# One encoder step on one core: a planner in the kernel sets the order of issue on all five engines

## The chip, the cores and the metric

The kernel runs as one program on one core of a Trainium2 chip. The metric is device time in microseconds of one execution, lower is better. Engines: PE (matrix), DVE (vector), ACT (scalar, activation functions), POOL (general, element-wise here), SP (only issues DMAs). Each works through its own queue in the order in which it was filled; an instruction that waits holds up those behind it on that engine.

## The reference, cut to what matters

One layer of a streaming encoder over 2048 prompt and 32 sample tokens (2080 columns in the kernel), model width 1024, fp32:

```
h  = RMSNorm(x);  qa,ka,va, qb,kb,vb, g,r = split(h @ w_in)
oa = band_attention(qa, ka, va)         # 8 heads x 64, own 64-token chunk and 8 before it, learned bias
ob = GLA(qb, kb, vb, sigmoid(g @ w_alpha2)^(1/16))   # 4 heads, state 64 x 128, serial in time
x += RMSNorm(concat(oa, RMSNorm(ob) * silu(r)) @ w_o)
x += RMSNorm(cross_attention(RMSNorm(x), 256 memory tokens, 4 heads x 256))
x += RMSNorm((silu(h @ w_gate) * (h @ w_up)) @ w_down)     # hidden 2816
```

Outputs are x and the new caches (the last keys and values, the GLA state, memory keys and values).

## The kernel before

Activations are feature-major (features on partitions, tokens along the row). Each fp32 operand is split into a rounded part (ACT cast, `split`, L77) and a rest (subtract on DVE or POOL, L81); a product is then three matmuls (`mm3`, L136). The large products work on 2 x 2 blocks with seven products in place of eight: operands are combined first (`sub` and `add`, L180 and L183: `seven_mov` for activations, `seven_sta` for weights), and a *unit* accumulates the seven products in three PSUM banks X, Y and Z. X is read out after each of its products by an ACT copy or a DVE add (`out`, L222, which only raises the priority):

```
prod(X, w[0], m[0], True, True);  out(ACT.copy, cp[0], X)
prod(Y, w[1], m[1], True, True);  out(ACT.copy, cp[1], Y)
prod(X, w[2], m[2], False, True); out(ACT.copy, cp[2], X)
prod(Y, w[3], m[3], False, True); out(add, DVE, dst[0, 1], cp[2], Y)
```

Four phases follow one another, each with its own pools:

1. *Projection* (about 0 to 620 us of the profile): three token blocks, weights streamed (`wva`, `wvb`, `wqa`, `wka`, `wqb`, `wkb`, `wr`; `_r` is the loaded weight, `_s` its split), results stored to DRAM (`qd`, `kad`, `vad`, `vbd`, ...). Between them SP fills the unused rows of these with `ones` (L538) and `zero` (L545), and the bias table is made: `rb` is loaded (L549, L550), copied on DVE (L551) and expanded through DRAM (`biasd`, `fl`, `nbd`).
2. *Mixing* (620 to 1450): band attention in units (scores `s`, transposes `pt`, value products `po`), GLA in tiles of 128 tokens (`gla_tile`: `g_z` gate, `g_e` and `g_W` decay, `g_s` scores, `g_t`, `g_o` output, `g_st` state, `g_tt` transpose back, each step waiting for the one before), and the output projection of four blocks (`wops`, L991), which reads the attention result `om` back from DRAM (`od`). Memory keys and values and the first query product fill in.
3. *Cross attention* (1450 to 2030): five blocks of 416 tokens; `mqps` queries, `ms` scores (softmax on ACT and DVE, transposes `mpt`), `mpv` values, `mops` output projection, norm, then the feed-forward input `h2d` in DRAM.
4. *Feed-forward* (2030 to the end): three blocks of 2 x 348 or 346 tokens, in each 11 groups of a gate unit (`pg`), an up unit (`pu`) and the down product of the group before (`pdn`, L136, into the six PSUM banks that X, Y and Z use too), which DVE copies (first group, L222) or adds (L183) into `acc`. `acc` has two tiles for a block, and the pool has two buffers: a block's first copies need the buffers of the block before. When a block ends, `square` sums squares into `ssq` (ACT, DVE); `finish` of that block is run after the next block's first gate and up units: a matmul with ones (`n_ps`, L1540), Ln and Exp on ACT (`rstd_of`, L85 and L86, each with a table load), eight multiplies by gain and norm on DVE (L1547), eight adds of the residual on POOL, two stores of `y_t` (L1550). In the last group `ffn_ops` makes the next block's operands `mf`.

The program text says what runs; the order on each engine is set by the tile framework's scheduler (`schedule_with_timeline_sim=True`), which takes ready instructions by priority. The kernel shapes it with `tc.high_priority(offset=...)` around loads and splits (`PRI` = 4000), with `out` and with `weave`, which mixes lists of steps in the program.

## Time and profile before

| | us |
|---|---|
| runs (3), median | 3518.83 (3514.37 to 3520.55) |
| the profiled execution, its own time | 3519.91 |
| its span, first to last instruction | 3518.1 |
| PE busy / DVE / ACT / POOL | 3230.3 / 2258.6 / 1705.1 / 1541.9 |
| mean granted clock of PE | 0.956 |

In a line of the trace stand the start, the busy time of the group, engine, line, operation, output <- inputs, shapes and count, and in brackets how long the engine was idle before it and what released it. Names in the profile leave numbers out: `g_tt` is the g_tt of any tile, `n_ps` any block's. A window's clock is the mean granted clock of PE in it.

### The profile page before, as it was taken

The numbers are of one execution on the slowest core, as the hardware profiler recorded it, in microseconds if no ns is written. First come the engines' busy times: TensorE is split into PE (matmuls) and PEld (weight loads), VectorE is DVE, ScalarE is ACT, GpSimd is POOL, SyncE is SP. The second block draws the span as 40 slices with busy tenths as digits, with TensorE's granted clock in tenths as the row PEclk, the third lists the DMA queues.
The fourth block names the chain that finished last, engine by engine and source line by source line (L and its number), as shares of the span: only waits on it lengthen the run. The fifth ranks groups of instructions, "written<-read, shape, count | busy, mean of one in ns | idle before, by whom it ended". The sixth has DMA issues, their size and how long they took to land.

```text
span 3518.1 us, 58416 instructions
## 1 busy us (share of the span) xinstructions
PE 3230.3 (92%) x21387; PEld 3070.5 (87%) x21387; DVE 2258.6 (64%) x4089; ACT 1705.1 (48%) x3719; POOL 1541.9 (44%) x1331
## 2 busy tenths in 40 slices
PE   7788899899999799879999879999989999899998
PEld 6788899788887578869999769999989999899998
DVE  7774855576676567266566686555875556865555
ACT  4554645566665366345455443333543334543334
POOL 4543533353445445553434453333454334543332
PEclk8999999899999799989999989999999999999999
DMA  5448364877585566874655542222342222332222
GB/s 141 156 127 283 110 183 134 255 241 249 158 283 167 167 209 193 287 223 119 208 186 176 164 158 72 73 72 79 99 137 73 73 72 86 99 91 79 72 73 89
DMA packets 520112, 520.42 MB, mean 148 GB/s; under 512 B 81936, under 2 KB 450745, under 8 KB 519825
## 3 DMA queue, kind: packets, MB, share of 16 engines
q1 hardware_dynamic: 519825, 516.70, 47.5%
q8 instruction: 168, 2.75, 0.3%
q14 instruction: 119, 0.97, 0.1%
HBM read 386.82 MB, written 130.87 MB: 147 GB/s over the span
## 4 chain that ended last, share of the span: by engine, by line
PE 62%; DVE 11%; DMA 5%; ACT 3%; issue 3%; POOL 2%; SPq 1%; DVEq 0%; POOLq 0%; ACTq 0%
PE pdn L136 13%; PE pg_X L136 6%; PE pu_X L136 6%; PE mops L136 5%; PE wops L991 4%; PE pu_Y L136 3%; PE pg_Y L136 3%; PE po L715 2%; PE mqps L136 2%; PE pu_Z L136 2%; PE pg_Z L136 2%; PE s L710 1%; PE ms L136 1%; DVE y L1349 1%; PE mpv L136 1%
## 5 line engine op out<-in xcount | busy, mean ns | idle before, releaser
L136 PE MATMUL pdn<-u,wd 128*128 128x346 f32 (+1 forms) x3168 | 525.0, 323 | 12.6 <-DVE acc L183 9.6
L136 PEld LDWEIGHTS pdn<-u,wd 128*128 128x128 f32 x3168 | 509.0, 190 | 14.6 <-DVE acc L183 10.7
L77 ACT CAST wg_s<-wg_r 128x512 fp32r<-128x512 f32 x231 | 139.3, 620 | 341.2 <-PE pdn L136 194.9
L183 DVE TENSOR_TENSOR acc<-acc,pdn 128x346 f32<-128x346 f32 (+1 forms) x464 | 233.3, 512 | 97.4 <-PE pdn L136 97.2
L136 PE MATMUL pg_X<-mf,wg_s 128*128 128x346 f32 (+1 forms) x1584 | 280.0, 326 | 16.8 <-ACT wg_s L77 16.2
L136 PE MATMUL pu_X<-mf,wu_s 128*128 128x346 f32 (+1 forms) x1584 | 285.9, 324 | 10.1 <-DVE up L183 9.5
L136 PEld LDWEIGHTS pg_X<-mf,wg_s 128*128 128x128 f32 x1584 | 261.0, 192 | 18.9 <-ACT wg_s L77 17.0
L81 POOL TENSOR_TENSOR wu_s<-wu_r,wu_s 128x512 fp32r<-128x512 f32 x132 | 174.5, 1323 | 233.2 <-ACT wu_s L77 209.7
L136 PEld LDWEIGHTS pu_X<-mf,wu_s 128*128 128x128 f32 x1584 | 260.8, 191 | 11.8 <-DVE up L183 10.9
L81 POOL TENSOR_TENSOR u<-sg,u 128x346 fp32r<-128x346 f32 (+1 forms) x132 | 151.9, 1161 | 236.0 <-ACT u L77 236.0
L991 PE MATMUL wops<-om,wo_s 128*128 128x512 f32 (+1 forms) x960 | 216.5, 378 | 25.5 <-DMA om<-od 11.2
L81 POOL TENSOR_TENSOR wg_s<-wg_r,wg_s 128x512 fp32r<-128x512 f32 x99 | 136.1, 1376 | 233.4 <-ACT wg_s L77 233.3
L136 PE MATMUL mops<-mo,wmo_s 128*128 128x416 f32 x960 | 200.2, 360 | 15.0 <-ACT mo L1320 6.7
L991 PEld LDWEIGHTS wops<-om,wo_s 128*128 128x128 f32 x960 | 165.0, 204 | 54.6 <-DMA om<-od 11.9
L136 PEld LDWEIGHTS mops<-mo,wmo_s 128*128 128x128 f32 x960 | 180.1, 192 | 21.7 <-ACT mo L1320 7.7
L77 ACT CAST wu_s<-wu_r 128x512 fp32r<-128x512 f32 x231 | 136.4, 619 | 65.9 <-DVE wu_r L183 36.2
L136 PE MATMUL mqps<-m,wmq_s 128*128 128x416 f32 x768 | 161.5, 359 | 5.9 <-DVE wmq_s L81 5.9
L715 PE MATMUL po<-prt,v 128*128 128x128 f32 x1120 | 159.7, 286 | 6.6 <-ACT prt L744 4.3
L715 PEld LDWEIGHTS po<-prt,v 128*128 128x128 f32 x1120 | 147.5, 200 | 14.8 <-ACT prt L744 4.8
L81 DVE TENSOR_TENSOR wg_s<-wg_r,wg_s 128x512 fp32r<-128x512 f32 x132 | 102.3, 776 | 86.4 <-ACT wg_s L77 86.4
L136 PE MATMUL pu_Y<-mf,wu_s 128*128 128x346 f32 (+1 forms) x792 | 141.3, 327 | 14.3 <-ACT wu_s L77 14.3
L136 PEld LDWEIGHTS mqps<-m,wmq_s 128*128 128x128 f32 x768 | 143.3, 191 | 9.5 <-DVE wmq_s L81 6.9
(476 smaller groups left out, 7892.4 us busy)
## 6 DMA issues: line engine op xcount, KB each, us to landing
wg_r<-in_w_ffn_gate_dram SPq DMA_DIRECT2D x66, 512.0 KB, 4.4
wu_r<-in_w_ffn_up_dram SPq DMA_DIRECT2D x66, 512.0 KB, 3.8
wd_r<-in_w_ffn_down_dram SPq DMA_DIRECT2D x66, 512.0 KB, 3.5
wmq_r<-in_w_mq_dram SPq DMA_DIRECT2D x80, 256.0 KB, 2.9
wmo_r<-in_w_mo_dram SPq DMA_DIRECT2D x80, 256.0 KB, 3.2
q<-qd SPq DMA_DIRECT2D x32, 512.0 KB, 5.0
wo_r<-in_w_o_dram SPq DMA_DIRECT2D x64, 256.0 KB, 3.6
om<-od SPq DMA_DIRECT2D x24, 512.0 KB, 8.5
```

The costliest lines, as they stand in the source:

```text
L77: ACT.copy(hi, src)
L81: lo_eng.tensor_tensor(out=lo, in0=src, in1=hi.bitcast(F32), op=ALU.subtract)
L136: PE.matmul(ps, lhsT=a, rhs=b, start=first and i == 0, stop=last and i == len(seq) - 1, skip_group_check=skip)
L183: eng.tensor_tensor(out=out, in0=a, in1=b, op=ALU.add)
L710: PE.matmul(ps_out, lhsT=q[:, 2 * i + e, q0 : q0 + nq], rhs=ks[:, e, k0 : k0 + ncol], start=i == 0, stop=i == 1)
L715: PE.matmul(po[:, e * P : e * P + n], lhsT=v[:kk, j, e * 64 : e * 64 + P], rhs=prt[:kk, j, :n], start=j == 0, stop=j == len(rows) - 1)
L991: PE.matmul(ps, lhsT=a, rhs=b, start=i == 0, stop=i == len(seq) - 1)
L1349: DVE.scalar_tensor_tensor(out=y[k], in0=y[k], scalar=gains["g_post_mem"][:, k : k + 1], in1=r, op0=ALU.mult, op1=ALU.mult)
```

## The change

A class `Order` is added and called twice: it is made when the pools are opened, and `queue()` runs at the end of the program. It reads the traced instructions with their tiles, gives each a price by engine and size, and works out what each needs: earlier writers and readers of the same cells, a free buffer of its tag, the release of pools whose room is taken over. A pass then plays all five engines against each other: whenever an engine is free it takes the ready instruction of highest priority. The first pass uses the program's priorities; after each pass a backward pass works out how late each instruction could run, and this is the next priority; of four passes the one that ends first by its own clock is kept. Last, each engine's instructions (SP's DMAs too) are chained in the order of their planned starts by dependencies that need no semaphore, so the framework's scheduler has no choice left. The instructions themselves stay as they are. Table loads of ACT are in no price, DVE and POOL are priced alone, and PE always at one clock. All lines after the class move down by 327 (L1547 becomes L1874, L136 L463, L81 L408).

```diff
+class Order:
+    ENGINES = ("PE", "Activation", "DVE", "Pool", "SP")
+    GATE = 5
+    SLOW = 1.1
+    PASSES = 3
...
+    def _cost(self, ins, kind, eng, outs, inps):
+        n = self._free(outs[0])
+        slow = self.SLOW
+        if eng == "PE":
+            if any(a.tensor.name.startswith(("ident", "anti")) for a in inps):
+                return (max(30.0, n * 0.86) if n < 128 else 110.0), 250.0
+            if any(a.dtype == F32 for a in inps):
+                if n <= 64 and list(inps[0].ap)[0][1] <= 64:
+                    return 82.0, 300.0
+                return 2 * max(n * 0.84, 60.0 if n < 128 else 108.0), 300.0
+            t = n * 0.4385 + 6.5
+            return (max(t, 111.0 if n >= 128 else 60.0) if n < 256 else t), 250.0
+        if eng == "SP":
+            return 450.0, 2200.0
+        if kind == "InstMemset":
+            t = 60 + n * 0.5
+        elif eng == "Activation":
+            if kind == "InstActivation":
+                t = 170 + n * 0.9 + (195 if len(outs) > 1 else 0)
+            else:
+                t = 165 + n * (0.87 if outs[0].dtype == F32R else 0.82)
+        elif eng == "Pool":
+            t = 170 + n * 2.35
+        elif kind == "InstTensorCopy":
+            t = 150 + n * 1.05
+        elif kind == "InstTensorTensor":
+            t = 200 + n * 1.15
+        elif kind == "InstTensorReduce":
+            m = self._free(inps[0])
+            t = 60 + m * (1.95 if m > 2 * n else 1.0)
+        elif kind == "InstReciprocal":
+            t = 130 + n * 6.4
+        elif kind == "InstTensorScalarPtr":
+            t = 120 + n * 0.83 if len(inps) < 3 else (230 + n * 1.75 if n > 256 else 200 + n * 1.4)
+        else:
+            t = 245 + n * 1.05
+        return t * slow, 90.0
...
+    def _pass(self, prio, back=None):
...
+            again = True
+            while again:
+                again = False
+                for e, heap in enumerate(ready):
+                    while idle[e] and heap:
+                        _, i = heappop(heap)
+                        stop = None
+                        for k in self.uses[i]:
+                            g = self.tag[k]
+                            if not held[k] and (free[g] <= 0 or head[g] != place[k] or (back is None and self.first[k] != i)):
+                                stop = g
+                                break
...
+                        idle[e] = False
+                        start[i] = now
+                        fin = now + dur[i]
+                        heappush(events, (fin, 0, i))
+                        if back is None:
+                            seen = fin + lat[i]
+                            if e == 4:
+                                moved = max(moved, fin) + self.size[i] / 300.0
+                                seen = max(fin + 1900.0, moved + 1300.0)
+                            end[i] = seen
+                            heappush(events, (seen, 1, i))
+                        else:
+                            end[i] = fin
...
+    def queue(self):
+        self._read(self.block.bb.instructions)
+        n = len(self.ops)
+        best = None
+        prio = self.prio
+        for turn in range(self.PASSES + 1):
+            start, end = self._pass(prio)
+            if best is None or max(end) < best[0]:
+                best = (max(end), start)
+            if turn == self.PASSES:
+                break
+            back, fin = self._pass([-(s + d) for s, d in zip(start, self.dur)], back=end)
+            whole = max(fin)
+            prio = [whole - b for b in fin]
+        start = best[1]
+        tail = {}
+        for i in sorted(range(n), key=lambda i: (start[i], i)):
+            e = self.eng[i]
+            if e == self.GATE:
+                continue
+            if e in tail:
+                self.tc.add_manual_dep(self.ops[i], self.ops[tail[e]].name, self.edge, reason="order of issue")
+            tail[e] = i
...
     RW = dict(reuse_waits="tile")
 
+    issue_order = Order(tc)
     PRI = 4000
...
                 finish_rows(0, xts)
 
+    issue_order.queue()
```

Three places show what moves. First PE where GLA tile 11 ends and the output projection of token block 2 begins (names: g11_tt is the last transpose of tile 11; wops1_7 the last of eight column blocks of block 1; s, pt and po with numbers 10 to 13 are band attention). Before:

```order
L975 MATMUL g11_tt_13132<-ident_61,g11_ob_12971 128x128 x4
L895 MATMUL g12_e18_13165<-tall_6191,g12_laR_12851 128x128 x2
L1021 MATMUL sqa_1_ps0_13196<-acc1_1_11331,ones_63 128x512
L917 MATMUL g12_s0_13233<-g12_W0_12920 64x64
L922 MATMUL g12_s0_13233<-g12_W0_12920 64x64 x12
L922 MATMUL g12_s0_13233<-g12_kq_12643 64x64 x2
L917 MATMUL g12_s1_13234<-g12_W0_12920 64x64
L922 MATMUL g12_s1_13234<-g12_W0_12920 64x64 x12
L922 MATMUL g12_s1_13234<-g12_kq_12643 64x64 x2
L991 MATMUL wops2_0_0_13779<-om2_4_13668,wo2_0_4_s_13776 128x512 x3
```

In the new order the end of wops1_7, band attention and tile 12 stand around g11_tt:

```order
L1318 MATMUL wops1_7_0_12949<-om1_3_11325,wo1_7_0_s_12941 128x512
L1037 MATMUL s11_7_1_13114<-ks10_3_12758,q10_3_12756 128x320 x2
L1222 MATMUL g12_e10_13103<-tall_6191,g12_laR_12851 128x512 x2
L1222 MATMUL g12_e14_13107<-tall_6191,g12_laR_12851 128x512
L1037 MATMUL s12_0_0_13154<-ks12_0_13045,q12_0_13043 128x320 x2
L1222 MATMUL g12_e14_13107<-tall_6191,g12_laR_12851 128x512
L1042 MATMUL po10_3_13096<-prt10_6_13074,v10_3_12759 128x128
L1069 MATMUL pt10_7_0_13123<-ident_61,u10_7_sb_12989 128x128 x3
L1037 MATMUL s12_0_1_13157<-ks12_0_13045,q12_0_13043 128x320 x2
L1069 MATMUL pt10_7_3_13128<-ident_61,u10_7_sb_12989 128x128
L1302 MATMUL g11_tt_13132<-ident_61,g11_ob_12971 128x128 x4
L1069 MATMUL pt10_7_3_13128<-ident_61,u10_7_sb_12989 128x128
```

Before, tile 11 comes well after all of wops1, and with eight rows between them wops2 begins; now tile 11 ends right behind wops1_7, and the first wops2 stands 44 rows after g11_tt.

Second SP in the projection, from the second load of weight unit wka1_0 (the rb loads are the bias table). Before (the 8x384 load of rb stands further up):

```order
L336 DMA wka1_0_r1_2810<-in_w_fm_dram 128x1024
L457 DMA vad1_83<-wva1_st0_2091 128x2x64 x2
L538 DMA vad1_83<-ones_2422 512x1x64 x6
L538 DMA vad2_84<-ones_2422 512x1x64 x6
L538 DMA vad2_84<-ones_2422 128x1x64
L545 DMA qd0_67<-zero_2441 64x512
L478 DMA glow1_98<-wva1_low_2378 16x768
L545 DMA qd0_67<-zero_2441 64x512 x3
L336 DMA wka1_1_r0_2971<-in_w_fm_dram 128x1024
```

```order
L336 DMA wka1_1_r1_2973<-in_w_fm_dram 128x1024
L545 DMA qd1_68<-zero_2441 64x768 x7
L545 DMA qd2_69<-zero_2441 64x800 x7
L336 DMA wqb1_r0_3134<-in_w_fm_dram 128x1024
L545 DMA qd2_69<-zero_2441 64x800
L550 DMA rb_2467<-in_rel_rev_dram 8x1
```

Now (the second load of wka1_0 stands three rows, five stores of ones, further up):

```order
L865 DMA vad2_84<-ones_2422 512x1x64 x3
L865 DMA vad1_83<-ones_2422 512x1x64
L865 DMA vad2_84<-ones_2422 128x1x64
L872 DMA qd0_67<-zero_2441 64x512 x8
L872 DMA qd1_68<-zero_2441 64x768 x8
L872 DMA qd2_69<-zero_2441 64x800
L663 DMA wka1_1_r0_2971<-in_w_fm_dram 128x1024
L872 DMA qd2_69<-zero_2441 64x800 x2
L876 DMA rb_2467<-in_rel_rev_dram 8x384
L877 DMA rb_2467<-in_rel_rev_dram 8x1
L872 DMA qd2_69<-zero_2441 64x800 x5
L663 DMA wka1_1_r1_2973<-in_w_fm_dram 128x1024
```

The stores of ones and zeros go out in one stretch, the rb loads stand in it, and the two loads of wka1_1 behind most of it. On DVE the copy of rb now stands in the splits of wka1_0 (before, it stood in those of wka1_1):

```order
L507 TENSOR_TENSOR wka1_0_r0_2808<-wka1_0_r1_2810,wka1_0_r0_2808 128x4x128
L878 COPY rb_2467<-rb_2467 8x382
L815 SCALAR_TENSOR_TENSOR ql1_0_2602<-wqa1_0_st_2503,qh1_0_2601 128x768
L408 TENSOR_TENSOR wka1_0_s2_2821<-wka1_0_r0_2808,wka1_0_s2_2821 128x512
L507 TENSOR_TENSOR wka1_0_r0_2808<-wka1_0_r1_2810,wka1_0_r0_2808 128x4x128
```

So what DVE does for wka1_0 comes after rb has landed.

Third DVE at the change from feed-forward block 0 to block 1 (acc0_1 and acc0_0 are block 0's sums, n5_0_1_r its norm; pu1_0 and pu1_1 the first two up units of block 1, pdn1_0 its first down product). Before, all eight multiplies stand in one row in the first unit's reads:

```order
L81 TENSOR_TENSOR wg1_1_s0_27601<-wg1_1_r0_27597,wg1_1_s0_27601 128x512
L180 TENSOR_TENSOR wg1_1_r0_27597<-wg1_1_r0_27597 128x4x128
L183 TENSOR_TENSOR wg1_1_r0_27597<-wg1_1_r0_27597,wg1_1_r1_27599 128x4x128
L1547 SCALAR_TENSOR_TENSOR acc0_1_22591<-acc0_1_22591,g_post_ffn_849,n5_0_1_r_27563 128x348 x8
L180 TENSOR_TENSOR wg1_1_r0_27597<-wg1_1_r1_27599,wg1_1_r0_27597 128x4x128
L183 TENSOR_TENSOR up1_0_01_27290<-pu1_0_c2_27456,pu1_0_Y_27452 128x346
L1481 TENSOR_TENSOR sg1_0_01_27286<-sg1_0_01_27286,up1_0_01_27290 128x346
L81 TENSOR_TENSOR wg1_1_s2_27610<-wg1_1_r0_27597,wg1_1_s2_27610 128x512
```

Now they come one group later, right ahead of the first copies into block 1's sums:

```order
L1874 SCALAR_TENSOR_TENSOR acc0_1_22591<-acc0_1_22591,g_post_ffn_849,n5_0_1_r_27563 128x348
L510 TENSOR_TENSOR ssq0_0_27205<-ssq0_0_27205,sq0_0_5_27259 128x348
L1874 SCALAR_TENSOR_TENSOR acc0_1_22591<-acc0_1_22591,g_post_ffn_849,n5_0_1_r_27563 128x348 x2
L510 TENSOR_TENSOR ssq0_0_27205<-ssq0_0_27205,sq0_0_6_27270 128x348
L1874 SCALAR_TENSOR_TENSOR acc0_1_22591<-acc0_1_22591,g_post_ffn_849,n5_0_1_r_27563 128x348
L510 TENSOR_TENSOR ssq0_0_27205<-ssq0_0_27205,sq0_0_7_27281 128x348
L1874 SCALAR_TENSOR_TENSOR acc0_1_22591<-acc0_1_22591,g_post_ffn_849,n5_0_1_r_27563 128x348 x3
L507 TENSOR_TENSOR wg1_2_r0_28043<-wg1_2_r0_28043 128x4x128
L1808 TENSOR_TENSOR sg1_1_10_27593<-sg1_1_10_27593,pu1_1_X_27755 128x346
L1874 SCALAR_TENSOR_TENSOR acc0_0_22590<-acc0_0_22590,g_post_ffn_849,n5_0_0_r_27867 128x348 x5
L549 COPY acc1_1_27285<-pdn1_0_0_1_27908 128x346
```

The multiplies of acc0_1 are spread over the reads of pu1_1, and five of acc0_0 stand ahead of the first copy of pdn1_0.

213 lines of the change are left out of this document (added).

## Prediction

> **What bounds the kernel now.** I read the page's first part and the chain of waits, then busy time and granted clock by stretch, then the timeline of the places where PE stands still.
>
> ```profile
> PE 3230.3 (92%) x21387; PEld 3070.5 (87%) x21387; DVE 2258.6 (64%) x4089; ACT 1705.1 (48%) x3719; POOL 1541.9 (44%) x1331
> PE 62%; DVE 11%; DMA 5%; ACT 3%; issue 3%; POOL 2%; SPq 1%; DVEq 0%; POOLq 0%; ACTq 0%
> ```
>
> PE is busy for 3230.3 of 3518.1 us, and 62% of the chain that ended last lies on it. A different order can win only what PE does not use: 287.8 us without work, and time in which its clock is not granted in full. The stretches follow the program's phases (in a row: length, busy PE, PEld, DVE, ACT, POOL, clock, DMA share, GB/s).
>
> ```profile
> 0.00:310.00 310.00, 244.75 (x1596) 230.91 (x1597) 213.82 (x266) 149.88 (x287) 134.90 (x88) 0.90 0.56 163
> 310.00:620.00 310.00, 299.13 (x1874) 292.37 (x1873) 197.87 (x255) 166.28 (x308) 133.78 (x89) 0.98 0.52 162
> 620.00:1144.00 524.00, 483.37 (x4211) 425.32 (x4209) 346.50 (x990) 320.21 (x857) 237.07 (x319) 0.95 0.71 225
> 1144.00:1232.00 88.00, 63.53 (x454) 46.81 (x455) 51.67 (x116) 31.91 (x92) 40.15 (x55) 0.77 0.53 166
> 1232.00:1450.00 218.00, 196.27 (x1516) 170.31 (x1515) 133.02 (x345) 126.81 (x339) 115.49 (x125) 0.94 0.72 226
> 1450.00:2024.00 574.00, 519.99 (x2964) 493.15 (x2962) 346.73 (x574) 290.80 (x661) 249.43 (x180) 0.96 0.60 185
> 2024.00:2112.00 88.00, 66.83 (x354) 61.67 (x355) 72.26 (x86) 43.69 (x78) 46.59 (x32) 0.85 0.49 158
> 2464.00:2640.00 176.00, 158.31 (x947) 155.51 (x946) 141.71 (x186) 83.88 (x152) 92.57 (x65) 0.95 0.39 118
> 2904.00:3080.00 176.00, 158.43 (x948) 155.69 (x947) 138.57 (x186) 84.54 (x153) 90.97 (x64) 0.95 0.31 93
> 3432.00:3518.00 86.00, 71.73 (x454) 70.79 (x452) 46.38 (x78) 35.86 (x73) 22.66 (x19) 0.93 0.28 91
> ...
> sum 968.00, PE 968.00 PEld 968.00 DVE 570.08 ACT 371.28 POOL 378.31; mean PE 322.67 PEld 322.67 DVE 190.03 ACT 123.76 POOL 126.11
> ```
>
> Length minus busy PE is idle; busy times one minus the clock is about what the clock costs. Idle, then clock: 65.3 and 24 (0:310), 10.9 and 6, 40.6 and 24, 24.5 and 15 (1144:1232), 21.7 and 12, 54.0 and 21 (1450:2024), 21.2 and 10, 17.7 and 8 (2464:2640), 17.6 and 8 (2904:3080), 14.3 and 5. That is some 288 us idle and 133 us of clock. The last row sums the steady feed-forward groups (2112:2464, 2640:2904, 3080:3432): PE is busy for 968.00 of 968.00 us. Over a quarter of the span can give nothing, only lose.
>
> **The change part by part.** No work is added or removed; what moves is the place of each instruction in its queue, so every term is a wait that shrinks, stays or is new.
>
> *GLA beside w_o (1144:1232).* Rows: start, length, then what ended the wait.
>
> ```profile
> 1157.60 0.60 PE L975 MATMUL g_tt<-ident,g_ob 128*128 128x128 f32 x4
> 1183.49 0.60 PE L975 MATMUL g_tt<-ident,g_ob 128*128 128x128 f32 x4
> 1196.01 2.99 PE L991 MATMUL wops<-om,wo_s 128*128 128x512 f32 x6 [7.80 <-DMA om<-od]
> ```
>
> The last transposes of GLA tiles 10 and 11 (g_tt) are 1183.49 − 1157.60 = 25.9 us apart, and in that stretch PE has hardly anything but this serial chain: matmul, Exp, mask, matmul. After tile 11 the result goes through DRAM (od, then om), and the first w_o product of block 2 starts 1196.01 − 1183.49 = 12.5 us later; PE has 31 matmuls in between and then waits 7.80 us. In the new PE queue the z matmul of tile 10 stands in w_o's third column block of block 1 instead of at the end of its fifth, g11_z in the fourth instead of behind the seventh, and between g11_tt and wops2 stand 125 matmuls, most of them band attention. So tiles 10 and 11 run inside w_o and band work that before was spent earlier. Floor of the gain: 0, if dense work merely runs out later. Ceiling: the 39 us of idle and clock. I take 28: at the stretch's mean of 63.53/454 = 0.14 us the 125 matmuls are 17 us, but half of them are 64 wide and shorter, so I count 9 and leave 3 of the 12.5 us open; the other 8 are short waits inside the tiles.
>
> The same shift goes through 620:1144 and 1232:1450, where the tiles' waits are 1 to 5 us each. Bounds: 0 and 65, 0 and 34 us (a loss is the slower rival's). I take 12 and 8, a fifth to a quarter: the GLA chain stays serial, and the other waits there are for DMAs whose sources do not move.
>
> *Entry of cross attention.*
>
> ```profile
> 1573.36 0.61 PE L1308 MATMUL mpt<-ident,mpr 104*128 104x104 f32 x2 [7.08 <-ACT prT L1309]
> 1581.77 1.06 PE L136 MATMUL mops<-mo,wmo_s 128*128 128x416 f32 x2 [5.05 <-ACT mo L1320]
> ```
>
> Score matmuls (ms) of block 0 stand some 4 to 10 us of PE work further ahead of w_mo's first product than before. These two waits are 12.1 us; softmax in front of them stays. I take 10 here and 5 from the rest of 1450:2024, where the other blocks move less; bounds 0 and 30.
>
> *Projection, 0:310.* Here the new order also does harm.
>
> ```profile
> 247.35 0.46 SPq L336 DMA_DIRECT2D wka_r<-in_w_fm_dram  x1
> 248.91 11.13 SPq L538 DMA_DIRECT2D vad<-ones  x13
> 267.58 11.93 SPq L545 DMA_DIRECT2D qd<-zero  x14
> 281.00 0.49 SPq L550 DMA_DIRECT2D rb<-in_rel_rev_dram  x1
> 264.75 0.69 DVE L180 TENSOR_TENSOR wka_r<-wka_r,wka_r 128x512 f32<-128x512 f32 x1 [2.13 <-POOL wka_s L81]
> 285.00 0.35 DVE L551 COPY rb<-rb 8x382 f32<-8x382 f32 x1 [7.43 <-DMA rb<-in_rel_rev_dram]
> 291.44 4.21 PE L136 MATMUL wka_Z<-mi,wka_s 128*128 128x384 f32 x12 [10.72 <-DVE wqa_st L183]
> ```
>
> DVE's copy of rb waited 7.43 us for a load that SP issued behind ones and zero stores, and PE then stood for 10.72 us. Thirteen ones took 11.13 us, fourteen zeros 11.93: 0.85 us each. The planner prices every SP entry at 450 ns. In the new SP queue both rb loads follow the second wka_0 load by 29 such stores: 247.35 + 29 × 0.85 + about 1 = 273 us, and landing took 4 us here (281.00 to 285.00): 277. But the copy now stands on DVE right behind a subtract that ran at 264.75, one weight unit earlier than before. So DVE would wait up to 277 − 266 = 11 us, ahead of the wka_0 lows. At the planner's 0.45 us the load lands near 265 and nothing waits. Between −4 (wait grows) and +14 (gone with its clock); I take +3, nearest to "as long as before". For the start and the other waits of 0:310 (about 50 us, from weight splits that arrive late) I take 12; together 15. 310:620 has 10.9 us in crumbs: 0.
>
> *Change of feed-forward block (2464:2640 and 2904:3080).*
>
> ```profile
> 2491.97 1.21 PE L136 MATMUL pdn<-u,wd 128*128 128x348 f32 x6 [2.38 <-DVE up L183]
> 2496.46 3.85 PE L136 MATMUL pdn<-u,wd 128*128 128x348 f32 x12 [3.28 <-DVE acc L183]
> 2544.13 0.75 PE L1540 MATMUL n_ps<-ssq,ones 128*128 128x348 f32 x2
> 2544.65 1.28 ACT L85 ACT_TABLE_LOAD   x1
> 2541.22 0.43 ACT L222 COPY pu_c<-pu_X 128x346 f32<-128x346 f32 x1
> 2538.16 0.68 DVE L180 TENSOR_TENSOR wu_r<-wu_r,wu_r 128x512 f32<-128x512 f32 x1
> 2548.34 8.46 DVE L1547 SCALAR_TENSOR_TENSOR acc<-acc,g_post_ffn,n_r 128x348 f32<-128x348 f32 x8 [2.26 <-ACT n_r L86]
> 2550.52 9.57 POOL L183 TENSOR_TENSOR acc<-acc,x2r 128x348 f32<-128x348 f32 x8
> 2556.73 1.43 DVE L180 TENSOR_TENSOR wg_r<-wg_r,wg_r 128x512 f32<-128x512 f32 x1
> 2562.44 3.35 PE L136 MATMUL pu_X<-mf,wu_s 128*128 128x346 f32 x12 [3.93 <-DVE up L183]
> 2583.65 3.57 PE L136 MATMUL pu_Y<-mf,wu_s 128*128 128x346 f32 x11 [6.87 <-ACT wu_s L77]
> 2589.14 2.08 PE L136 MATMUL pu_X<-mf,wu_s 128*128 128x346 f32 x12
> out_dram<-acc SPq DMA_DIRECT2D x4, 696.0 KB, 4.6
> ```
>
> Two blocks of eight gain multiplies on DVE (8.46 us the first) hold up PSUM evacuation, and PE waits 3.93 and 6.87 us; 2.38 and 3.28 us went earlier, where the next block's operand splits stand ahead of the last adds. In the new DVE queue the splits lie between the accumulate adds: I take those 5.7 us as won (bounds 0 and 5.7). The multiplies, though, come a whole group later: n5_0_1_ps leaves pu1_0_Z for pu1_1, a few rows before the first copy of pdn1_0 into acc1_1, and this tile takes over the buffer of acc0_1 (two buffers), which is free only when that block's result is written out. Count from n_ps: two table loads and two activations 3.7 us (2544.65 to 2548.34); eight multiplies 8.46 with ten other entries between them, at the 0.68 of a plain one some 6 more; last POOL add 9.57/8 = 1.2; store to landing 4.6: 24 us. PE has after n_ps 48 matmuls of pu1_1 and 36 of pdn1_0 until six PSUM buffers are full: 84 × 0.16 us (12 in 1.9 us) = 13.4. So PE waits about 10 us at pdn1_0, where before it waited 10.8 in two pieces. The second change is alike. Net: 5.7 less about 1 for what I cannot see: 5 each, bounds −6 (the new wait half as long again) and +20 (no wait, with its clock).
>
> The planner knows no table load; the row has 1.28 us. The Trainium skill (ScalarE: Activation LUTs, What ACT_TABLE_LOAD costs) puts a switch at 2.66 us with its drain; two of those would be 5.3 us, and the late chain would cost 1.6 us more at each change. The 3.7 us above hold two switches and two activations, so the rows decide.
>
> *Entry of the feed-forward part* (21.2 us idle): the chain norm, h2d store and load, split is serial in both orders: 2, bounds 0 and 8. *End* (14.3): same chain, 0. *Steady groups*: whole products of twelve in the order X0 Y1 X2 Y3 X4 Z X6; an evacuation of X has 12 matmuls, 1.9 us, of cover, and the copy takes 0.43 (2541.22): 0, only downwards.
>
> Sum: 28 + 12 + 8 + 15 + 15 + 10 + 2 = 90 us. Against the profiled 3519.9 us (1.1 above the median shown): 3430.
>
> **The rivals.** *More*: the planner sees slots, pools and all queues, so the idle of the five stretches before 2024 outside 310:620 (206 us, with 96 of clock) falls by more than half: −170, 3350. For it: the prices fit PE (twelve in 1.9 us). Against it: chains through DRAM and softmax stay serial.
>
> *Nothing*: terms of the size of the rb and acc waits turn up in each stretch, because a list order fixed on wrong SP, table and POOL prices stops a queue at its head where another entry was ready; they eat the 90: 3515 to 3527. For it: both such waits above come out of the order itself.
>
> *DVE and POOL in each other's way*: the planner prices each alone. The DVE subtract of 512 columns took 0.68 us at 2538.16 and 1.43 at 2556.73, under POOL's adds. If each of some 16 DVE entries of the late chain loses 0.75 us, both changes lose 12: the sum is 66, 3454. The Trainium skill (SBUF — State Buffer, Who interferes with whom) speaks for this: a DVE instruction with two SBUF inputs and a GpSimd one that reads SBUF exclude each other for a whole instruction; these two rows agree. Against it: the planner's prices for plain DVE entries stand above 0.68, and at most changes of order the two engines have gaps.
>
> *Slower*: the steady groups. There are 33, each with 2 × 84 + 96 matmuls, 42 us at 100%. DVE is 59% busy there (570.08 of 968), POOL 39%, and the new order no longer slips the Z product between Y and X. If a PSUM copy or a u split stands behind something late, each group pays. 90/33 = 2.7 us a group is where the sum turns; 4 us would give 3519.9 − 90 + 132 = 3562. Against it: 1.9 us of cover against 0.4.
>
> **How the numbers follow.** Forecast 3430, chance 0.46, own range 3390 to 3475. More 0.20, in each other's way 0.10, nothing 0.08 (0.05 within 0.2%, 0.02 below, 0.01 above), slower 0.16. The range takes the middle of More, and ends where Nothing ends: 3350 to 3520. About 0.2% (7 us) is what these runs tell from no change. Faster: 0.46 + 0.20 + 0.10 + 0.02 = 0.78; same 0.05; slower 0.17.
>
> **What would show it.** Right: in the stretch where GLA tile 11 ends PE idle falls from 24.5 to near 6 and the wait before the first wops2 is under 4 us; at each block change one wait of 5 to 12 us before pdn1_0, released by DVE's copy into acc; steady windows still at 88 of 88. The rb step is right if DVE waits at the copy for 5 to 11 us, wrong if the copy finds its data. Wrong altogether: PE below 98% in steady windows (slower), or idle below 150 us in all (more).

## Result, and the profile after

The changed kernel takes 3418.43 us (median of 4 runs, 3413.63 to 3419.78), the kernel before 3519.35 (4 runs, 3514.37 to 3520.55): a ratio of 0.9713, 95% interval 0.9697 to 0.973. The forecast was 3430 in a range of 3350 to 3520. The profiled execution took 3413.63 us with a span of 3411.8.

The four phases, cut at the first score matmul of band attention, the first of cross attention and the first gate matmul. First the windows before, then after (length, busy PE, PEld, DVE, ACT, POOL, clock, DMA share, GB/s):

```profile
0.00:629.10 629.10, 552.98 (x3546) 532.15 (x3547) 413.51 (x525) 317.63 (x597) 269.14 (x180) 0.94 0.54 163
629.10:1503.30 874.20, 780.98 (x6433) 679.56 (x6432) 542.63 (x1464) 498.92 (x1321) 419.25 (x514) 0.93 0.70 220
1503.30:2031.80 528.50, 473.08 (x2632) 447.16 (x2630) 340.59 (x562) 270.54 (x624) 226.87 (x160) 0.96 0.58 180
2031.80:3518.10 1486.30, 1423.30 (x8780) 1411.66 (x8780) 961.88 (x1539) 618.03 (x1178) 626.66 (x478) 0.98 0.29 88
```

```profile
0.00:613.00 613.00, 547.11 (x3545) 524.09 (x3546) 429.59 (x525) 316.86 (x597) 271.03 (x180) 0.96 0.56 168
613.00:1440.50 827.50, 771.63 (x6414) 666.58 (x6413) 546.09 (x1463) 503.20 (x1319) 413.02 (x512) 0.96 0.73 232
1440.50:1937.40 496.90, 466.56 (x2653) 445.22 (x2651) 350.07 (x562) 275.88 (x626) 240.23 (x161) 0.98 0.61 192
1937.40:3411.80 1474.40, 1419.90 (x8780) 1402.96 (x8780) 1011.76 (x1540) 618.46 (x1177) 630.15 (x479) 0.99 0.29 89
```

| | length before | after | won | forecast |
|---|---|---|---|---|
| projection | 629.1 | 613.0 | 16.1 | 15 |
| mixing | 874.2 | 827.5 | 46.7 | 48 |
| cross attention | 528.5 | 496.9 | 31.6 | 15 |
| feed-forward | 1486.3 | 1474.4 | 11.9 | 12 |

Together the four phases won 106.3 us of span, where the terms of the forecast make 90. The borders are not quite those of the forecast, whose windows began at 620, 1450 and 2024 us: the stretch from 1450 to 1503.3, 6.4 us of it idle, stood in its cross attention and stands here in mixing.

Length minus busy PE: idle time of PE fell from 287.8 to 206.6 us, and its busy time by 25.1 us to 3205.2, as the mean clock rose from 0.956 to 0.974. DVE is busy 79 us longer with the same number of instructions (4089).

Finer stretches of the changed kernel:

```profile
1110.00:1200.00 90.00, 81.84 (x619) 65.41 (x617) 67.38 (x168) 56.37 (x147) 46.93 (x52) 0.98 0.77 243
...
2018.00:2370.00 352.00, 352.00 (x2210) 352.00 (x2210) 221.60 (x366) 136.73 (x267) 140.68 (x111) 1.00 0.25 76
2370.00:2546.00 176.00, 158.03 (x963) 154.78 (x962) 145.96 (x192) 82.99 (x149) 89.67 (x65) 0.96 0.38 115
...
2854.00:3030.00 176.00, 162.20 (x983) 158.56 (x982) 148.85 (x195) 83.79 (x151) 91.95 (x66) 0.95 0.33 101
...
3338.00:3412.00 74.00, 63.84 (x392) 61.87 (x390) 39.49 (x68) 32.27 (x66) 18.57 (x16) 0.93 0.30 92
```

In the first block's steady groups PE is busy for 352.00 of 352 us; the two others have 308.00 of 308: 968 of 968 us, as before. Tile 11 (1110:1200) leaves 8.2 us idle at a clock of 0.98, where its stretch had 24.5 us and 0.77.

Three places on the timeline of the changed kernel: the bias table (SP, DVE, PE), the first w_o product of block 2, and the first change of block (PE, then POOL and DVE):

```profile
241.39 8.55 SPq L865 DMA_DIRECT2D vad<-ones  x10
249.99 12.13 SPq L872 DMA_DIRECT2D qd<-zero  x17
264.27 0.55 SPq L876 DMA_DIRECT2D rb<-in_rel_rev_dram  x1
268.60 0.35 DVE L878 COPY rb<-rb 8x382 f32<-8x382 f32 x1 [11.27 <-DMA rb<-in_rel_rev_dram]
270.47 4.46 PE L463 MATMUL wka_X<-mi,wka_s 128*128 128x384 f32 x12 [5.99 <-DVE wka_s L408]
...
1139.34 0.50 PE L1318 MATMUL wops<-om,wo_s 128*128 128x512 f32 x1
...
2490.24 0.88 PE L1867 MATMUL n_ps<-ssq,ones 128*128 128x348 f32 x2 [3.86 <-DVE ssq L510]
2494.79 2.10 PE L463 MATMUL pdn<-u,wd 128*128 128x346 f32 x6 [3.67 <-DVE sg L1808]
2501.76 9.20 PE L463 MATMUL pdn<-u,wd 128*128 128x346 f32 x48 [4.87 <-DVE acc L549]
2513.17 2.18 PE L463 MATMUL pdn<-u,wd 128*128 128x346 f32 x12 [2.21 <-DVE acc L549]
...
2487.03 2.34 POOL L510 TENSOR_TENSOR acc<-acc,x2r 128x348 f32<-128x348 f32 x2 [0.46 <-DVE acc L1874]
2487.37 1.23 DVE L510 TENSOR_TENSOR ssq<-ssq,sq 128x348 f32<-128x348 f32 x1
2489.67 0.51 DVE L510 TENSOR_TENSOR ssq<-ssq,sq 128x348 f32<-128x348 f32 x1
2496.74 4.53 DVE L1874 SCALAR_TENSOR_TENSOR acc<-acc,g_post_ffn,n_r 128x348 f32<-128x348 f32 x5 [2.01 <-ACT n_r L413]
2501.20 2.21 DVE L549 COPY acc<-pdn 128x346 f32<-128x346 f32 x5
2512.59 1.79 DVE L549 COPY acc<-pdn 128x346 f32<-128x346 f32 x4 [0.91 <-DMA out_dram<-acc]
```

DVE waited 11.27 us at the copy of rb, and PE 5.99 behind it. The first w_o product of block 2 waits for nothing (7.80 us before). At the change PE waits in four pieces, 14.6 us together; at the second change its waits of over 2 us make 11.7.

### The profile page after: what moved, and what is told of

The parts are those of the page before. It is cut to its first block, busy times and chain, and to the rows that moved or that the text cites. A ratio compares the mean times of both kernels' runs of the same rounds, so it can differ in the third digit from the quotient of the medians.

```text
span 3411.8 us, 58315 instructions
## 1 busy us (share of the span) xinstructions
PE 3205.2 (94%) x21387; PEld 3038.8 (89%) x21387; DVE 2337.5 (69%) x4089; ACT 1714.4 (50%) x3717; POOL 1554.4 (46%) x1331
## 5 line engine op out<-in xcount | busy, mean ns | idle before, releaser
L463 PE MATMUL pdn<-u,wd 128*128 128x346 f32 (+1 forms) x3168 | 516.6, 323 | 20.4 <-DVE acc L549 12.8
L463 PEld LDWEIGHTS pdn<-u,wd 128*128 128x128 f32 x3168 | 508.9, 190 | 24.3 <-DVE acc L549 14.3
L408 POOL TENSOR_TENSOR wu_s<-wu_r,wu_s 128x512 fp32r<-128x512 f32 x132 | 195.4, 1488 | 272.2 <-ACT wu_s L404 244.9
L463 PE MATMUL pg_X<-mf,wg_s 128*128 128x346 f32 (+1 forms) x1584 | 279.7, 324 | 16.5 <-ACT wg_s L404 12.0
L463 PE MATMUL pu_X<-mf,wu_s 128*128 128x346 f32 (+1 forms) x1584 | 276.4, 322 | 6.1 <-DVE up L510 4.2
L463 PEld LDWEIGHTS pg_X<-mf,wg_s 128*128 128x128 f32 x1584 | 257.4, 190 | 21.2 <-ACT wg_s L404 12.3
L408 POOL TENSOR_TENSOR wg_s<-wg_r,wg_s 128x512 fp32r<-128x512 f32 x99 | 135.8, 1374 | 301.7 <-ACT wg_s L404 298.1
L463 PEld LDWEIGHTS pu_X<-mf,wu_s 128*128 128x128 f32 x1584 | 255.9, 189 | 8.0 <-DVE up L510 4.8
L463 PE MATMUL mops<-mo,wmo_s 128*128 128x416 f32 x960 | 197.1, 356 | 5.9 <-DVE y L1662 5.1
L463 PEld LDWEIGHTS mops<-mo,wmo_s 128*128 128x128 f32 x960 | 179.2, 190 | 10.6 <-issue 7.3
L1318 PEld LDWEIGHTS wops<-om,wo_s 128*128 128x128 f32 x960 | 153.5, 194 | 32.9 <-ACT wo_s L404 7.0
L408 POOL TENSOR_TENSOR u<-sg,u 128x346 fp32r<-128x346 f32 (+1 forms) x132 | 141.5, 1083 | 90.1 <-ACT u L404 86.3
L463 PE MATMUL mqps<-m,wmq_s 128*128 128x416 f32 x768 | 165.3, 358 | 0.0
L463 PE MATMUL pu_Y<-mf,wu_s 128*128 128x346 f32 (+1 forms) x792 | 140.0, 323 | 3.3 <-ACT wu_s L404 2.8
L463 PEld LDWEIGHTS mqps<-m,wmq_s 128*128 128x128 f32 x768 | 140.2, 190 | 2.9 <-issue 1.3
L408 POOL TENSOR_TENSOR wd<-wd_r,wd 128x512 fp32r<-128x512 f32 x66 | 89.1, 1351 | 114.8 <-ACT wd L404 111.9
```

Of the source, the lines that this page charges most:

```text
L408: lo_eng.tensor_tensor(out=lo, in0=src, in1=hi.bitcast(F32), op=ALU.subtract)
L463: PE.matmul(ps, lhsT=a, rhs=b, start=first and i == 0, stop=last and i == len(seq) - 1, skip_group_check=skip)
L1318: PE.matmul(ps, lhsT=a, rhs=b, start=i == 0, stop=i == len(seq) - 1)
```

## The experiments

**One part of the program at a time.** The planner works as before, but only the instructions of one phase are chained; the rest is left to the framework's scheduler. For feed-forward:

```diff
-    def queue(self):
+    def queue(self, lo=0, hi=10 ** 9):
...
-            if e == self.GATE:
+            if e == self.GATE or not lo <= at[self.ops[i].name] < hi:
                 continue
...
-    issue_order.queue()
+    issue_order.queue(marks[2])
```

(`marks` holds the places in the program where mixing, cross attention and feed-forward begin; the two other runs take the pieces between them.)

> Only the instructions of the mixing part are chained in the planned order (GLA tiles inside w_o and band attention). Theory A: the time falls by 40 to 52 us (46.8 in the whole change), and the wait of 7.80 us before wops of block 2 is gone. Rival B: under 30 us, because the part begins with the old projection's loads and the framework's order of the borders.

> Only the instructions of cross attention are chained in the planned order. The whole change saved 31.5 us between the first ms and the first pg, twice what was forecast. Theory A (that part's own order closes its waits for softmax, prT and mo): the time falls by 25 to 36 us, the waits of 7.08 and 5.05 us at the entry are gone. Rival B (the gain comes from the mixing part, which ends with the first cross-attention queries already made): under 15 us, and the entry waits stay.

> Only the instructions of the feed-forward part are chained in the planned order; the other three parts are left to the framework's scheduler. Theory A (each part's order pays by itself, and what the whole change saved after the first pg, 11.9 us, is that part's own): the time falls by 8 to 16 us, nearly all at the two changes of block. Rival B (a part gains only because the part before hands over earlier and with fuller buffers): within 5 us of before, or the entry of the part gets longer.

| chained | us | ratio (interval) | projection | mixing | cross attention | feed-forward |
|---|---|---|---|---|---|---|
| mixing | 3472.93 | 0.9863 (0.9849 to 0.9878) | 632.3 | **829.3** | 523.8 | 1487.9 |
| cross attention | 3500.85 | 0.9943 (0.9928 to 0.9957) | 629.9 | 875.5 | **501.4** | 1491.5 |
| feed-forward | 3516.32 | 0.9984 (0.9975 to 0.9994) | 630.6 | 879.0 | 525.9 | **1481.2** |

Mixing wins 44.9 us and cross attention 27.1 by their own order, with nothing inherited from the phase ahead. For mixing that is Theory A; the 7.80 us wait is gone. For cross attention the phase itself and the two entry waits came out as in Theory A, but in the whole program the gain is 18.7 us, between the two theories, mainly because the feed-forward part behind it, not chained, took 5.2 us more. Feed-forward alone wins 5.1 of 11.9 us, and the whole program 3.2: Rival B. Its entry is most of the difference: a pu unit there waits 5.38 us for DVE (1.75 in the full change), and pg units wait 3.03 and 1.56, while the waits at the first change are those of the full change to within 0.7 us. The 5.1 us is itself uncertain, since phases left to the scheduler came out up to 5 us from the old profile (mixing 879.0 for 874.2).

**One engine alone, one engine less, no backward pass.** The line that skips an engine is the edit (`e != 0` chains PE alone, `e in (4, self.GATE)` all but SP); the third sets `PASSES = 0`, so the plan by the program's priorities is kept.

> Only PE is chained in the planned order; DVE, ACT, POOL and SP are ordered by the framework around it. Theory A (PE's order, GLA ahead of dense work, is the change; the others follow it by need): 60 to 100 us faster than before. Rival B (a fixed PE queue without the matching order of the engines that feed it stands at its head): less than 30 us faster, or slower than before, with PE waits for DVE and ACT spread over all parts.

> The planned order on PE, DVE, ACT and POOL; SP's DMAs are left to the framework's scheduler, which has to serve these queues. Theory A (SP's order is a small part; rb and the loads find a place by need): 80 to 105 us faster than before. Rival B (fixed compute queues make a DMA that is issued late cost its whole delay, as in the run with PE alone): under 60 us faster, with waits for DMA in mixing and projection.

> The planner with PASSES = 0: one forward pass with the program's own priorities, no latest-start priorities. Theory A (the forward model of slots, queues and prices does most of it, since program order already puts GLA tiles early enough once all engines are played together): 60 to 100 us faster than before. Rival B (the priorities from the backward pass are what moves the GLA chain and the loads ahead): less than 30 us faster than before, or slower.

| | us | ratio (interval) | projection | mixing | cross attention | feed-forward |
|---|---|---|---|---|---|---|
| PE alone | 3566.53 | 1.0136 (1.0115 to 1.0157) | 638.9 | 888.8 | 514.8 | 1517.9 |
| all but SP | 3450.13 | 0.9798 (0.9777 to 0.9819) | 623.8 | 844.6 | 502.2 | 1475.9 |
| no backward pass | 3492.13 | 0.9916 (0.989 to 0.9941) | 630.1 | 838.5 | 509.4 | 1509.4 |

One row of the PE timeline, first with PE alone, then with no backward pass:

```profile
653.03 1.19 PE L1202 MATMUL g_z<-wal,g_ga 17*128 17x256 f32 x2 [8.04 <-DMA g_kq<-qbd]
```

```profile
2539.56 1.53 PE L1867 MATMUL n_ps<-ssq,ones 128*128 128x348 f32 x2 [9.00 <-DVE ssq L510]
```

The same PE order that is 2.9% faster with the other queues is 1.4% slower without them: PE stands at the head of its queue for what the others do later, here 8.04 us for a load that SP had not made yet (Rival B). SP's order alone is worth 32 us, nearly all of it ahead of feed-forward; the 74 us that are left without it lie between the two theories. The plan by the program's priorities wins 54 us ahead of feed-forward and loses 23 in it, part of them where the norm's matmul waits 9.00 us for `ssq`; it is 32 us faster than the kernel before, close to Rival B's bound of 30, and the backward passes are worth 74 us.

**The rb loads.** A first edit meant to move the two loads selected no instruction, so this run repeats the changed kernel's order and tests neither theory. It shows how far the same order varies.

> The planned order with one edit: the two SP loads of rb are issued ahead of the first store of ones in place of behind 29 stores of ones and zeros. In the changed kernel DVE's copy of rb waited 11.27 us, and the next PE wait was 5.99 us. Theory A (that wait comes from the planner's SP price alone): DVE's copy finds its data, the 5.99 us are gone, and the projection part is 5 to 9 us shorter than in the changed kernel (613 us), the time near 3411. Rival B (the wka_1 loads behind the same stores are late as well): the projection part is within 2 us of 613, and the wait stands at wka_1 instead.

Measured: 3418.15 us, 0.9698 (0.9674 to 0.9722), a span of 3423.3 in the profile; its parts 616.2, 834.0, 498.0 and 1475.1 are up to 7 us from those of the changed kernel's profile. Part times are read with that in mind. Then the edit that moves them:

```diff
         start = best[1]
+        moved = [i for i in sp if dst(i, r"rb(_\d+)?$")]
+        for i in moved:
+            start[i] = first - 1.0
```

(`sp` are SP's entries, `first` is the start of the first store of ones.)

> The two loads of rb are queued on SP ahead of the first store of ones; all else keeps the changed kernel's order. Theory A (wrong SP price): the copy of rb no longer waits on DVE (11.27 us in the changed kernel, 10.28 in its repeat), and the PE wait behind it (5.99 and 5.01 us) falls below 2; the projection is 4 to 6 us shorter (613.0 to about 608), the whole about 3413, 0.15% below the changed kernel. Rival B (the weight loads behind the same fills end the wait next): DVE does not wait at the copy, but PE waits 4 us or more for the next weight unit, and the projection stays at 612 to 614. Rival C (own price): the PE wait is gone, and later parts give the gain back: projection 608, whole 3418.

Measured: 3418.17 us, 0.9706 (0.9693 to 0.9719); projection 616.9. SP, DVE and PE:

```profile
232.31 0.61 SPq L885 DMA_DIRECT2D rb<-in_rel_rev_dram  x1
253.61 12.12 SPq L881 DMA_DIRECT2D qd<-zero  x17
260.78 0.34 DVE L887 COPY rb<-rb 8x382 f32<-8x382 f32 x1
272.59 0.62 PE L472 MATMUL wka_X<-mi,wka_s 128*128 128x384 f32 x2 [2.83 <-ACT wka_s L413]
277.27 0.81 SPq L889 DMA_DIRECT2D biasd<-rb  x1
282.09 1.03 SPq L895 DMA_DIRECT2D fl<-biasd  x2
288.32 2.47 PE L902 MATMUL flp<-fl,anti 128*128 128x320 f32 x4 [6.60 <-DMA fl<-biasd]
```

The copy no longer waits, and PE's wait behind it falls from 5.99 to 2.83 us. But the next step of the same chain, the store of biasd, still stands on SP behind the zeros (277.27, before the edit 274.62), and PE then waits 6.60 us for `fl`: the first flp product starts at 288.32 us, in the changed kernel at 285.61. The wait has moved along the chain and the gain is zero: Rival B's outcome by another transfer than it named.

**The late work at a block change.** The squares, sums and norm get 25 us more urgency after each backward pass:

```diff
             prio = [whole - b for b in fin]
+            for i, ins in enumerate(self.ops):
...
+                if any(re.match(r"n5_|ssq\d_|sq\d_\d_\d", a.tensor.name) for a in aps):
+                    prio[i] -= 25000.0
```

> The planned order, with the priority of the end-of-block work of the feed-forward part (squares, sums of squares, norm, gain multiplies) moved 25 us ahead of the planner's latest start; everything else by the same rules. In the changed kernel PE waits 14.6 us at the first change of block and 11.7 at the second. Theory A (latest-start priorities place this work just in time, and prices without table loads and without DVE and POOL in each other's way make it late): these waits fall to under 6 us each, 10 to 18 us in all, the time near 3404. Rival B (DVE has too much to do there in any order): the waits only move to the reads of the first gate and up units, and the time is within 5 us of the changed kernel's.

Measured: 3421.58 us, 0.9709 (0.9692 to 0.9726). The feed-forward window, a stretch of 4 us in the change, and PE around it:

```profile
1941.80:3416.10 1474.30, 1427.16 (x8780) 1409.18 (x8780) 1010.36 (x1541) 620.61 (x1179) 634.47 (x479) 0.98 0.29 89
...
2478.00:2482.00 4.00, 4.00 (x14) 3.61 (x13) 4.00 (x6) 0.48 (x1) 3.02 (x3) 0.50 0.86 299
```

```profile
2475.16 0.58 PE L468 MATMUL pg_X<-mf,wg_s 128*128 128x346 f32 x2 [1.79 <-DVE sg L515]
2477.41 1.53 PE L1872 MATMUL n_ps<-ssq,ones 128*128 128x348 f32 x2 [1.67 <-DVE ssq L515]
2487.45 3.25 PE L468 MATMUL pu_X<-mf,wu_s 128*128 128x346 f32 x10 [1.14 <-POOL wu_s L413]
```

Idle time of feed-forward fell from 54.5 to 47.1 us, and the part took 1474.3 against 1474.4: busy PE rose by as much. The long waits became several, of 1.1 to 1.8 us at the first change and up to 2.5 at the second, and ten matmuls behind them take 3.25 us, where in the steady stretch (352.00 us for 2210) ten take 1.6; the clock in the stretch between is 0.50, though PE is busy all the time. Laid over PE's rows, the clock records of the trace show some 37 us of busy time at half clock in this phase, 23 in the changed kernel: 7 us of work lost. So less idle time in small pieces was worth nothing here, which is Rival B in time. The sizes are uncertain: in the run with the rb loads moved, whose feed-forward order is that of the changed kernel, idle time is 51.2 us and half clock some 33, and the phase takes 1474.6. The Trainium skill (TensorE: Matmul & The Clock Gate, HAM oscillation — how this bites in real kernels) gives the rule that the clock falls after idle gaps longer than about 3.4 us; here gaps of 1.79 and 1.67 us, with 0.58 us of work between them, sufficed. Its section A second HAM failure mode: psum-queue depth-cycling tells of the clock falling by short and frequent idle gaps between groups of matmuls; with that these rows agree.

**The planner's prices.** Three runs: DVE's operations on two tensors (`InstTensorTensor`) at 1.4 times and POOL at 1.2 times the price; the same with 1280 ns for the norm's table loads and 850 ns for SP's stores of ones and zero; these last two alone.

```diff
-            t = 170 + n * 2.35
+            t = (170 + n * 2.35) * 1.2
...
-            t = 200 + n * 1.15
+            t = (200 + n * 1.15) * 1.4
```

```diff
-            return 450.0, 2200.0
+            fill = any(a.tensor.name.startswith(("ones", "zero")) for a in inps)
+            return (850.0 if fill else 450.0), 2200.0
...
+                if outs[0].tensor.name.startswith("n5"):
+                    t += 1280 / slow
```

> The planner's price of a DVE operation with two inputs is 1.4 times, of a POOL operation 1.2 times as high, about what the profile of the changed kernel shows while both work (0.51 to 1.23 us for the same DVE operation at a block change). Theory A (the planner's prices for two engines in each other's way cost time): the waits at the two block changes (14.6 and 11.7 us) fall by half, the feed-forward part is 8 to 12 us shorter (1474 to 1464), the whole about 3405. Rival B (the clock takes it back, as when the late work was moved earlier): the feed-forward part stays within 3 us of 1474, the whole 3412 to 3425. Rival C (too high a price where POOL rests): mixing or projection is 5 us or more longer, the whole over 3425.

> The prices of the run before, and two more from the profile: 1280 ns for the table load ahead of each activation of the norm (n5), and 850 ns in place of 450 for a store of ones or zero on SP. Theory A (wrong prices are what is left to win): the copy of rb waits under 3 us on DVE, the projection is 4 to 6 us shorter, the block changes as in the run before or better; the whole 3395 to 3405. Rival B: rb as in A, but the feed-forward part is unchanged and the other parts move either way by a few us; the whole 3410 to 3422. Rival C (a list order is chaotic in its prices: any change of prices reshuffles all parts by several us each): parts differ from the changed kernel's by 5 us or more in both directions with no link to what was priced anew.

> The changed kernel's DVE and POOL prices, and from the run with all prices only the two others: 1280 ns for a table load ahead of the norm's activations, 850 ns for a store of ones or zero on SP. It tells whether the 166 us lost there came from the DVE and POOL prices alone. Theory A (they did, and the other two are right and worth something): the steady groups stay at 100% PE, the waits at each block change fall from 14.6 and 11.7 us to under 8, DVE does not wait 10 us at the copy of rb; the feed-forward part 1468 to 1472 (1474.4 in the changed kernel), the whole 3395 to 3411. Rival B (right prices where little hangs on them): each part within 5 us of the changed kernel's, the whole 3411 to 3425. Rival C (any other price breaks the order): PE under 98% in the steady groups, the whole over 3450.

| prices | us | ratio (interval) | projection | mixing | cross attention | feed-forward |
|---|---|---|---|---|---|---|
| DVE, POOL up | 3596.76 | 1.0212 (1.0198 to 1.0226) | 656.2 | 865.6 | 504.8 | 1569.1 |
| all four | 3583.9 | 1.0175 (1.0161 to 1.0189) | 646.0 | 876.2 | 503.2 | 1564.3 |
| table, SP | 3421.29 | 0.9724 (0.9711 to 0.9738) | 615.5 | 827.7 | 495.0 | 1475.7 |

The first is slower even than the kernel before. That is Rival C in direction, at many times its size, and no theory had expected feed-forward to lose most. A steady stretch in it, and PE in a steady group:

```profile
2114.00:2466.00 352.00, 345.10 (x2130) 338.16 (x2129) 229.00 (x346) 127.44 (x256) 143.59 (x104) 1.00 0.23 72
```

```profile
2275.68 0.48 PE L463 MATMUL pu_X<-mf,wu_s 128*128 128x348 f32 x2
2276.77 1.86 PE L463 MATMUL pu_X<-mf,wu_s 128*128 128x348 f32 x10 [0.61 <-POOL wu_s L408]
```

In 352 us it does 2130 matmuls where the changed kernel does 2210, 3.6% fewer, with waits that come back in each group; over the 968 us of steady groups that is some 35 us, and the rest of the 95 us lost in feed-forward lies in its entry, its end and the changes of block. In the order made for slow DVE and POOL the gate and up units are cut into pieces of 2 and 10 matmuls, and the splits of wu come just too late. The run with all four prices loses nearly as much, and fits none of its expectations: every phase is longer than in the changed kernel.

With the two other prices alone the steady groups are whole again, so the loss was that of the DVE and POOL prices (Theory A's first half). Where they act, the waits shrink:

```profile
270.82 0.35 DVE L881 COPY rb<-rb 8x382 f32<-8x382 f32 x1 [8.59 <-DMA rb<-in_rel_rev_dram]
...
2491.72 1.06 PE L1870 MATMUL n_ps<-ssq,ones 128*128 128x348 f32 x2 [3.29 <-DVE ssq L513]
2502.10 9.48 PE L466 MATMUL pdn<-u,wd 128*128 128x346 f32 x48 [2.34 <-DVE acc L552]
2513.90 2.19 PE L466 MATMUL pdn<-u,wd 128*128 128x346 f32 x12 [2.32 <-DVE acc L552]
```

PE's waits of over 2 us at the changes fall from 14.6 and 11.7 us to 8.0 and 7.0, but waits of 1 to 2 us, of which the changed kernel has none there, add 3.0 and 4.0; DVE waits 8.59 us instead of 11.27 for rb. The time does not follow (Rival B): feed-forward is at 1475.7. No run beat the changed kernel by more than the same order varies.

## Why the prediction held, and where its steps failed

The forecast was 12 us too high and the mechanism is the one described, waits of PE that shrink; the miss is nearly all in one term, cross attention.

**Mixing, 48 forecast, 46.7 measured.** The GLA term is right in mechanism: in the stretch of tile 11 idle fell from 24.5 to 8.2 us and the clock loss from 14.6 to about 2 (81.84 × 0.02), and the wait ahead of wops2 is gone. These make 29 us for 28, but the two stretches hold different work (454 and 619 matmuls), so that the size of this term and of the 12 and 8 beside it was not measured one by one. Over the whole phase idle time fell by 37.3 us and busy time by 9.4. The chain of mixing alone keeps 44.9 us. That this is the mechanism for the whole phase, not only for tile 11, is inferred from the idle time of the windows; no run took tile 11 alone.

**Cross attention, 15 forecast, 31.6 measured: the term that was mis-sized.** It lies just over the upper bound of 30, and the shifted borders do not explain it: they take 6.4 us of idle time out of the phase and bring 7.8 us in, as part of a wait before the first gate unit that hardly changed (12.26 us before, 11.99 after). The step that failed is "the other blocks move less". Groups of PE in the phase, before, then after (count, busy, mean ns, idle before them and what released it):

```profile
L136 PE MATMUL mops<-mo,wmo_s 128*128 128x416 f32 x960 | 200.2, 360 | 15.0 <-ACT mo L1320 6.7 <-DVE mo L1321 4.8 <-ACT wmo_s L77 2.7
L136 PE MATMUL mqps<-m,wmq_s 128*128 128x416 f32 x744 | 156.9, 360 | 5.9 <-DVE wmq_s L81 5.9
L1308 PE MATMUL mpt<-ident,mpr 104*128 104x104 f32 (+2 forms) x160 | 29.0, 261 | 14.4 <-ACT prT L1309 13.7 <-DVE mpr L1305 0.7
```

```profile
L463 PE MATMUL mops<-mo,wmo_s 128*128 128x416 f32 x960 | 197.1, 356 | 5.9 <-DVE y L1662 5.1 <-ACT mo L1647 0.7
L463 PE MATMUL mqps<-m,wmq_s 128*128 128x416 f32 x764 | 164.5, 358 | 0.0
L1635 PE MATMUL mpt<-ident,mpr 104*128 104x104 f32 (+2 forms) x160 | 28.8, 260 | 7.1 <-DVE mpr L1632 3.0 <-ACT prT L1636 2.6 <-DVE mst L1631 1.4
```

Idle time in front of these three groups fell from 35.3 to 13.0 us: 22 us, of which the two entry waits (7.08 and 5.05) can be 12 at most. The smaller waits behind them, before transposes, query products and output products, gained the rest, and the higher clock (0.96 to 0.98) some 6 us more. I had read only the two longest waits and counted the many of 1.5 to 5 us behind them as 5 us together.

**Projection, 15 forecast, 16.1 measured.** The rb step came out as worked: DVE waited 11.27 us (forecast up to 11) behind 29 stores, of which the 27 shown took 0.77 us each (0.85 forecast). Its price of +3 was a choice, and no run isolates it: DVE's wait grew from 7.43 to 11.27 us, yet PE's wait behind it fell from 10.72 to 5.99, and with DVE's wait removed the next transfer of the same chain took its place. Idle time of the phase fell by 10.2 us, 4.7 of them at this wait, and busy time by 5.9. With SP not chained the phase took 623.8 us, so two thirds of the gain hang on SP's order.

**Feed-forward, 12 forecast, 11.9 measured, right by luck: its terms are off in both directions.** The steady groups gave 0, as said. Both traces have 8780 PE matmuls in the phase, so the gain can be read part by part, at the same matmul in both. The entry gave 1.9 us (2 forecast). The changes gave some 2.5 and 5.5 (5 each): their windows of 176 us hold 963 matmuls for 947 and 983 for 948, at 0.16 us each. The end, put at 0 because its chain is the same, gave some 2: six norm matmuls (`nl_ps`) wait for the last sum as before, but transposes that were done ahead of the last down product now stand in that wait. PE before, then after:

```profile
3504.49 1.32 PE L1573 MATMUL nl_ps<-ones,ssq 128*128 128x1 f32 x6 [6.15 <-DVE ssq L183]
```

```profile
3398.81 1.28 PE L1900 MATMUL nl_ps<-ones,ssq 128*128 128x1 f32 x6 [0.31 <-DVE ssq L510]
```

From the end of the last down product to these matmuls it is 6.2 us before and 6.5 after; of the 24 transposes (`xtp`), 20 have come into that stretch.

In the changes the wait predicted before pdn1_0 is there (4.87 us, where 5 to 12 were named), but its cause is only half mine. I had made the copies into `acc` wait for the buffer. The first five (2501.20) came straight behind five multiplies which had waited 2.01 us for the norm on ACT: DVE's queue held them, and only four later ones (2512.59) waited for the store, 0.91 us. I also left out two waits ahead of it, 3.86 us for `ssq` and 3.67 for `sg`. In both DVE ran late, in part under POOL's adds: the same addition into ssq took 1.23 us at 2487.37, begun inside two of POOL's adds (2487.03 to 2489.37), and 0.51 at 2489.67, begun when none was running. That is the mechanism of the rival "in each other's way", priced there at 12 us for both changes. The changes still won 8 of the 10 us that I had counted; what this rival cost there no run isolates.

**The rivals.** *More* did not come: idle ahead of feed-forward fell by a third, not by half. *Nothing*'s single waits came (rb, acc) without the sum. *Slower* did not come by this change, but its mechanism is real and near: the same planner with DVE and POOL priced too high broke the steady groups by some 35 us, 1.1 a group, and with what the other phases lost it ended at 3597 us.

## What to carry to other kernels

An order for one engine is only as good as the queues that feed it: lay out all engines, DMA issue included, in one plan, since the same PE order alone made the kernel slower. Size a reordering by the sum of waits in the whole stretch, not by the two longest, and do not count idle time as won when it is only broken into small waits, which here cost as much again in clock. A price raised for the places where two engines work at once also changes the order where they do not: here it broke the dense steady part, though the places that it was meant for lie elsewhere.

## What the runs showed of the hardware

Waits of 1.1 to 1.8 us, one after another, took the clock down to 0.50 at the first change of block, and 7.4 us less idle time in feed-forward gave 0.1 us.

DVE's total rose by 79 us with the same instructions, 33 us of it in the steady feed-forward groups (570.08 us before, 221.60 + 190.83 + 190.62 after), where PE is full in both orders. What changed is what ran beside them. The same 33 operations on DVE, before, then after (duration in ns, lowest, median and highest):

```profile
L180 DVE TENSOR_TENSOR wu_r<-wu_r x33: 679/693/1149, 2056.7 to 3442.1; 128x512 f32<-128x512 f32 x33
```

```profile
L507 DVE TENSOR_TENSOR wu_r<-wu_r x33: 678/1408/1428, 1957.8 to 3336.4; 128x512 f32<-128x512 f32 x33
```

Laid over POOL's rows of the trace, they ran beside a POOL instruction for 2.8 us of 23.9 before, and for 38.5 us of 42.2 after. PE lost nothing by it in these groups.

A profile of one order differs from another of the same order by up to 7 us in a phase (mixing 827.5 and 834.0).
